# Spacing the steps of a side stream by their bytes, and six groups of an MLP block as seven half products

## The chip, the cores and the metric

The kernel runs on one core of a Trainium2 chip. The metric is the device time of one launch, in microseconds (us). Three runs of the kernel before took 3230.37, 3218.70 and 3221.98 us, a median of 3221.98.

## The reference

One inference step of a one-layer decoder. A prompt of 2048 tokens and 64 sampled tokens (8 sequences of 8) go through one input projection, two kinds of heads (softmax attention with forget gates, "fox", and a matrix memory, "mLSTM"), one output projection, a layer norm, an MLP and a second layer norm. The sampled tokens attend to 8192 cached positions per sequence, which lie in pages that a page table picks. All data are float32.

```python
z = x @ w_in                                     # 1024 -> 3600 columns: q, k, v, gates
fox = softmax(q k^T / 8 + forget sums) v         # prompt: causal; sampled: cache pages + new tokens
mix = concat(fox, mlstm) @ w_o
x1  = layer_norm(2**0.25 * x + mix)
hid = square(relu(x1 @ w1))                      # 1024 -> 4096
y   = layer_norm(2**0.25 * x1 + hid @ w2)        # 4096 -> 1024
```

## The kernel before

**Products.** A float32 product is made of three passes: both operands are split into a high part (ScalarE copy, line 149) and the rest (a subtraction, line 152, on VectorE unless another engine is named), and `mm3` (lines 157 to 159) issues high x high, low x high and high x low as three matmuls into the same sum. `mm2` (163, 164) is the form for the 64 sampled tokens, whose high and low parts lie side by side.

**Phases in order.** A: input projection in four blocks of 512 tokens, with the mLSTM beside it. B: prompt attention. O: output projection and first norm. C: the MLP.

**Phase C** goes through tokens in four blocks of 512 (`CB`); the last also has the 64 sampled tokens. A block goes through the 4096 hidden columns in 16 groups of 256. `hidden(fc)` computes one group's activations for the block (2 x 8 x 3 matmuls of 128x512, banks named `ph`), `output(fc)` multiplies the group before with its 256 rows of w2 (4 token tiles x 2 column halves x 2 x 3 matmuls of 128x512, banks named `py`) and VectorE adds every 128x512 result onto the running rows `y` (line 1638). Groups 14 and 15 are output together. Each group needs four 512 KB pieces of weights (`wr`, four buffers): two of w1, two of w2. The fourth block is done by `last_block` with `seven` (groups 0 to 13): the 512 x 256 activations and the 256 x 1024 weights are cut into halves each way, and the 2x2 product of halves is made from seven products instead of eight. One product is 2 token tiles x 3 matmuls of 128x512. `sums` builds sums and differences on GpSimd (lines 1714 to 1723), `build` splits them, and `output` adds each result to the quarters of `y` that it belongs to, on VectorE (1771 for the part that is shared and kept in `ac`, 1778 for the rest); `join` adds `ac` once at the end.

**The stream.** Attention of the sampled tokens to the cache (`sample_attention`) is a generator of 295 steps that runs beside phases A, O and C. Every matmul of the main work adds its nominal time to a counter by `tick`; when the counter passes a pace, one step is issued (`attend`). The pace is 5.6 in phase A (`PACE_A`), infinite in B (six gathers are issued there by hand), 5 in O and C (`PACE_C`). A step may hold: `k_gather` (512 KB of keys through an indirect DMA issued by GpSimd, line 2027), `k_turn` (two VectorE transposes, 2033), `qk_step` for every fourth step (32 small matmuls, `sQ`, 2056), a pair of `v_gather`s (2 x 512 KB of values, 2145) and `pv_step` (16 small matmuls, `sO`, 2169). Keys come in steps up to 255; from 35 on values come too, one pair per two steps; from 256 on, values alone. Steps up to NA+2 belong to phase A, with NA = 4 x GA and GA = 19, and use a ring of four key pieces; later ones use a ring of six. At most two pairs of values are held, one of them in the landing buffers `xr` of the MLP.

In the third block, after group 13's hidden part and group 12's output, whatever is left of the stream is issued at once, and `sampled()` follows: the output projection and first norm of the 64 sampled tokens, which needs the stream's result (`mhs` is its split input; products by `mm2`).

**Order.** The program order above is not the final one: a scheduler with its own timing model orders the instructions of each engine at build time. `tc.issue_after(x)` keeps what is issued under it behind x in that order.

## Time and profile before

| what | us |
|---|---|
| median of three runs | 3221.98 |
| the profiled execution | 3218.31 |
| its span, first to last instruction | 3216.6 |
| TensorE busy in it | 3159.1 |
| VectorE, ScalarE, GpSimd busy | 2202.3, 1381.0, 1013.6 |

The profile is of one execution. PE is TensorE's matmul side, PEld its weight loads, DVE is VectorE, ACT ScalarE, POOL GpSimd, SP the queue that issues most transfers. "L1638" is a line of the kernel. Matmuls overlap, so the shown duration of one (0.39 us for 128x512) is longer than its distance to the next; the distance is what it costs. In the span phase A lasts to about 890 us, B to about 1290, O to about 1530, the first three blocks of C to about 2810, the last to the end.

### The profile page before, as it was taken

The page shows a single profiled execution, that of the slowest core. Times are in us where ns is not written, and L with a number is a line of the kernel's source. Part 1 is how long each engine was busy: PE and PEld are TensorE (multiplying, and loading weights), DVE is VectorE, ACT ScalarE, POOL GpSimd, SP SyncE. Part 2 cuts the span into 40 slices and gives each one's busy share as a digit, 9 for nine tenths or more (in the row PEclk, how much of TensorE's full clock was granted, in tenths as well). Part 3 has the DMA queues.
Part 4 walks back from the last instruction along what each step waited for, and adds up shares of the span by engine and source line. Part 5 has one row for each costly group of instructions (what it writes and reads, how often), then busy time and mean ns, then how long its engine had stood idle before and what let it go on. Part 6 is the DMA issues. An engine that isn't in the chain of part 4 may idle for free.

```text
span 3216.6 us, 54583 instructions
## 1 busy us (share of the span) xinstructions
PE 3159.1 (98%) x20140; PEld 2546.2 (79%) x20140; DVE 2202.3 (68%) x5111; ACT 1381.0 (43%) x2675; POOL 1013.6 (32%) x1157
## 2 busy tenths in 40 slices
PE   9999999999999999999999999999999999999998
PEld 8988787787777777777777777777777777799997
DVE  6857667567577777776566667666676544787777
ACT  4444245345377777412333333233423333444443
POOL 0011122323244444354333223333233110164441
PEclk9999999999999999999999999999999999999999
DMA  6565775977642324688877768677678655432221
GB/s 192 163 193 174 226 225 172 311 253 236 213 133 86 80 85 118 235 308 281 293 254 251 252 243 309 249 247 253 238 263 295 206 175 168 149 132 83 89 92 56
DMA packets 413731, 641.86 MB, mean 200 GB/s; under 512 B 82908, under 2 KB 295200, under 8 KB 412568
## 3 DMA queue, kind: packets, MB, share of 16 engines
q1 hardware_dynamic: 337208, 360.99, 36.6%
q0 software_dynamic: 74304, 270.57, 22.7%
q10 hardware_dynamic: 1952, 6.82, 0.6%
q8 instruction: 159, 2.61, 0.3%
q14 instruction: 108, 0.88, 0.1%
HBM read 585.43 MB, written 52.83 MB: 198 GB/s over the span
## 4 chain that ended last, share of the span: by engine, by line
PE 37%; issue 7%; DMA 3%; POOL 2%; DVE 2%; ACT 0%; DVEq 0%; POOLq 0%; ACTq 0%
PE ph L159 6%; PE ph L157 6%; PE ph L158 6%; PE py L157 5%; PE py L159 5%; PE py L158 5%; DMA kT<-cache_k,idxK 3%; PE sO L2169 2%; PE sQ L2056 1%; POOL kT L2027 1%; DMA vt<-cache_v,idxV 1%; PE py L163 0%; PE py L164 0%; POOL vt L2145 0%; PE sT L2128 0%
## 5 line engine op out<-in xcount | busy, mean ns | idle before, releaser
L149 ACT ACTIVATE wh<-wr 128x1024 fp32r<-128x1024 f32 x268 | 277.8, 1056 | 537.9 <-PE py L159 254.4
L2027 POOL DMA_INDIRECT kT<-cache_k,idxK x256 | 265.6, 1037 | 733.0 <-PE sQ L2056 609.6
L2033 DVE STREAM_TRANSPOSE kT<-kT 128x512 f32<-128x512 f32 x512 | 329.4, 685 | 194.6 <-DMA kT<-cache_k,idxK 194.4
L157 PE MATMUL ph<-x1h,wh 128*128 128x512 f32 (+2 forms) x1280 | 453.1, 354 | 3.3 <-ACT x1h L149 1.9
L158 PE MATMUL ph<-x1l,wh 128*128 128x512 f32 (+2 forms) x1280 | 452.3, 354 | 1.0 <-DVE x1l L152 1.0
L159 PE MATMUL ph<-x1h,wl 128*128 128x512 f32 (+2 forms) x1280 | 450.6, 354 | 2.0 <-DVE wl L152 1.9
L152 DVE TENSOR_TENSOR wl<-wr,wh 128x1024 fp32r<-128x1024 f32 x252 | 308.5, 1233 | 81.9 <-PE ph L159 45.7
L157 PE MATMUL py<-wh,h 128*128 128x512 f32 (+1 forms) x888 | 348.2, 397 | 3.6 <-DVE y L1638 3.3
L158 PE MATMUL py<-wl,h 128*128 128x512 f32 (+1 forms) x888 | 347.6, 392 | 0.0
L159 PE MATMUL py<-wh,h 128*128 128x512 f32 (+1 forms) x888 | 346.4, 391 | 0.1
L1638 DVE TENSOR_TENSOR y<-y,py 128x512 f32<-128x512 f32 x336 | 223.0, 677 | 178.8 <-PE py L159 177.7
L157 PEld LDWEIGHTS ph<-x1h,wh 128*128 128x128 f32 x1280 | 241.5, 189 | 37.4 <-ACT x1h L149 2.1
L159 PEld LDWEIGHTS ph<-x1h,wl 128*128 128x128 f32 x1280 | 241.3, 189 | 36.6 <-DVE wl L152 3.2
L158 PEld LDWEIGHTS ph<-x1l,wh 128*128 128x128 f32 x1280 | 241.4, 189 | 36.4 <-issue 2.5
L2145 POOL DMA_INDIRECT vt<-cache_v,idxV x160 | 161.4, 1009 | 306.9 <-PE sO L2169 257.4
L157 PE MATMUL pm<-whi,xhT 128*128 128x512 f32 (+2 forms) x648 | 235.2, 365 | 2.5 <-DVE xlT L152 1.0
L158 PE MATMUL pm<-wlo,xhT 128*128 128x512 f32 (+2 forms) x648 | 229.6, 354 | 0.0
L159 PE MATMUL pm<-whi,xlT 128*128 128x512 f32 (+2 forms) x648 | 229.2, 354 | 0.0
L157 PEld LDWEIGHTS py<-wh,h 128*128 128x128 f32 x888 | 166.6, 188 | 50.3 <-issue 9.9
L159 PEld LDWEIGHTS py<-wh,h 128*128 128x128 f32 x888 | 166.7, 188 | 36.8 <-issue 2.1
L158 PEld LDWEIGHTS py<-wl,h 128*128 128x128 f32 x888 | 167.0, 188 | 32.3 <-issue 2.1
L149 ACT ACTIVATE whi<-wra 128x1024 fp32r<-128x1024 f32 (+1 forms) x112 | 119.0, 1062 | 150.6 <-PE pm L159 100.7
(490 smaller groups left out, 6965.8 us busy)
## 6 DMA issues: line engine op xcount, KB each, us to landing
wr<-w SPq DMA_DIRECT2D x256, 512.0 KB
wra<-w_in SPq DMA_DIRECT2D x112, 512.0 KB
Rb<-dR SPq DMA_DIRECT2D x128, 128.0 KB
wr<-w_o SPq DMA_DIRECT2D x16, 512.0 KB
xr<-dmix SPq DMA_DIRECT2D x16, 512.0 KB
y<-x_prompt SPq DMA_DIRECT2D x16, 512.0 KB
dx<-y SPq DMA_DIRECT2D x16, 512.0 KB
qn<-dq SPq DMA_DIRECT2D x120, 64.0 KB
```

Source lines behind the costliest of these rows:

```text
L149: last["ACT"] = A.activation(dst, src, AF.Copy, scale=scale)
L152: r = (eng or V).tensor_tensor(dst, src, hi.bitcast(F32), op=OP.subtract)
L157: T.matmul(ps, wh, xh, start=first, stop=False, skip_group_check=free)
L158: T.matmul(ps, wh, xl, start=False, stop=False, skip_group_check=free)
L159: last["PE"] = T.matmul(ps, wl, xh, start=False, stop=stop, skip_group_check=free)
L1638: V.tensor_tensor(y, y, ps, op=OP.add)
L2027: G.indirect_dma_start(out=piece(n), out_offset=None, in_=ck, in_offset=IO(ap=idxK[:, b, j // 2, j % 2:j % 2 + 1], axis=0))
L2033: V.transpose(x, x)
L2056: r = T.matmul(pq[h4 * 32:h4 * 32 + 32, hg].rearrange("p (k f c) -> p k f c", k=2, f=4), z["qb"][:, hd], kv, start=(db == 0), stop=(db == ...
L2145: vx["last"] = G.indirect_dma_start(out=vt.rearrange("p f c -> p (f c)"), out_offset=None, in_=cv, in_offset=IO(ap=idxV[:, b, (kt % 4) * 4 ...
L2169: after_ = T.matmul(po[r:r + 32], z["PT"][:, hg, 2 * f + g, pg].rearrange("p h q -> p (h q)"), vts[f][:, g, hg * 256:(hg + 1) * 256], star ...
```

## The change

Five things are changed.

1. *Spacing.* In phase A the pace is 3.6 while the step number is below 34 (`PACE_K`, keys alone) and 6.0 afterwards. GA is 21, so eight more steps (79 to 86) belong to phase A. From step 262 (`TAIL`) the pace is 2.3 (`PACE_T`), up to four pairs of values are held (the key ring's three places are used for them too), and a step gathers at most one pair more than is held.
2. *Where the stream must end.* The left-over steps are issued after group 6's hidden part and group 5's output in the third block instead of seven groups later; `sampled()` follows one group later.
3. *Seven products.* Groups 8 to 13 of the third block go through `seven`. Group 8's hidden part has both subtractions of w1 on VectorE (`eng` None); in groups 9 to 13 the second is on GpSimd.
4. *Banks.* From group 8 on, the third block's sums are in the six banks that before were opened by `last_block` (three pairs, `ppl`), its hidden part and the transposes at the seam to the last block are in the two banks `sX` and `sO` that the stream used.
5. *Small.* The first operations of phase B (`b_first`, on GpSimd) are placed behind the matmul issued last; the last addition of the sampled tokens' first norm is on VectorE, not GpSimd; an unused argument goes.

```diff
-PACE_A = 5.6
+PACE_A = 6.0
+PACE_K = 3.6
 PACE_C = 5
+SEVEN = 8
+PACE_T = 2.3
...
-        while acc[1] is not None and acc[0] > acc[2]:
-            acc[0] -= acc[2]
+        while acc[1] is not None and acc[0] > (pace := PACE_T if kx["tail"] else PACE_K if kx["keys"] else acc[2]):
+            acc[0] -= pace
             attend()
...
-                    b_first()
+                    with tc.issue_after(last["PE"].ins):
+                        b_first()
...
             for fc in range(16):
+                if ci == 2 and fc == SEVEN:
+                    break
...
-                if fc == 13 and ci == 2:
+                if ci == 2 and fc == SEVEN - 2:
                     while acc[1] is not None:
                         tick(100.0)
-                    sampled()
+            if ci < 2:
+                continue
+            run = seven(ph, blk, ys, C["x"], w2, lambda: es_l["ppl"])
+            sampled()
+            run["hidden"](SEVEN, None)
+            run["sums"](SEVEN)
+            output([SEVEN - 1])
+            es.close()
+            es_l["ppl"] = es_q.enter_context(tc.tile_pool(name="ppl", bufs=1, space=PSUM, reuse_waits="tile"))
+            for n in range(SEVEN + 1, 16):
+                if n < 15:
+                    h = run["build"](n - 1)
+                if n < 14:
+                    run["hidden"](n)
+                    run["sums"](n)
+                else:
+                    hidden(n, lambda f: pps.tile([128, 512], F32, name="ph", tag="sO" if f else "sX", bufs=1))
+                if n < 15:
+                    run["output"](n - 1, *h)
+                if n == 14:
+                    run["join"]()
...
+            load(3, px_of)
+            output([14, 15], True)
...
-    GA = 19
+    GA = 21
...
+    def v_place():
+        free = [0] + ([1] if vx["more"] else []) + ([2, 3, 4] if kx["tail"] else [])
+        return next((p for p in free if p not in vx["live"]), None)
...
-        if n > NA + 2:
+        if kx["tail"]:
+            pairs = min(len(vx["live"]) + 1, 4)
+        elif n > NA + 2:
             pairs = (2, 0, 1, 0)[n % 4]
...
+    TAIL = 262
...
+        kx["tail"], kx["keys"] = n >= TAIL, n < 34
         step(n)
```

More of the change, by code (lines that the diff above doesn't have):

```diff
@@ L105, in body @@
     vx = dict(more=None, live=[], next=0, of={})
-    kx = dict(ring=None, new=False, free=False)
+    kx = dict(ring=None, new=False, free=False, tail=False, keys=False)
     def take_back():
@@ L1623, in output @@
                     pss = []
+                    pair = es_l["ppl"].tile([128, 2, 512], F32, name="py", bufs=3) if wide else None
                     for hf, cs in enumerate(halves):
@@ L1626, in output @@
                             todo = halves if both else [cs]
-                            new = [ppc.tile([128, 512], F32, name="py", bufs=3) for _ in todo]
+                            new = [ppc.tile([128, 512], F32, name="py", bufs=3) for _ in todo] if pair is None else [pair[:, i] for i in range(2)][hf:hf + len(todo)]
                             pss += new
@@ L1663, in phase_c, with px_of @@
                         SY.dma_start(v, dap(I[f"ln2_{x}"], 0, [[0, 128], [1, D]]))
+            es_px.close()
+            C["px"] = es_px.enter_context(tc.tile_pool(name="px", bufs=1, reuse_waits="tile"))
+            C["w"] = 576
+            turn = [0]
+            def px_of():
+                turn[0] += 1
+                return pps.tile([128, 4, 128], F32, name="px2", tag="sO" if turn[0] % 2 else "sX", bufs=1)
+            load(3, px_of)
+            output([14, 15], True)
         es_h.close()
-        es.close()
-        last_block(w2, gb2)
+        last_block(w2, gb2, es_l["ppl"])
+        es_q.close()
         es_px.close()
@@ L2139, in v_gather @@
         vx["next"] += 1
-        place = 0 if 0 not in vx["live"] else 1
+        place = v_place()
         vx["live"].append(place)
```

42 lines of the change are left out of this document (20 added, 22 removed).

## The prediction

> **What bounds the kernel.** First I read the busy shares, then who TensorE waited for, then single stretches.
>
> ```profile
> span 3216.6 us, 54583 instructions
> PE 3159.1 (98%) x20140; PEld 2546.2 (79%) x20140; DVE 2202.3 (68%) x5111; ACT 1381.0 (43%) x2675; POOL 1013.6 (32%) x1157
> ```
>
> ```profile
> PE sO L2169 <- DMA vt<-cache_v,idxV: 4.6, 4, 2.4
> PE py L163 <- DVE mhs L152: 1.8, 1, 1.8
> PE ph L157 <- ACT wh L149: 1.4, 1, 1.4
> ```
>
> TensorE is without work for 3216.6 - 3159.1 = 57.5 us in all. The second view (who waits for whom: total, times, longest) shows that this is many small pieces; the whole stream costs it 4.6 us of waiting for values. So time comes from removed matmuls, almost one for one, and little else can come back. The stretches in which the third block and the end of the stream lie say the same (TensorE busy, then the other engines, clock, share of the DMA engines, GB/s):
>
> ```profile
> 2400.00:2480.00 80.00, 80.00 (x512) 61.81 (x511) 57.18 (x107) 28.77 (x40) 32.29 (x30) 1.00 0.93 339
> 2640.00:2720.00 80.00, 80.00 (x425) 62.87 (x424) 36.75 (x46) 24.32 (x33) 8.82 (x9) 1.00 0.53 176
> ```
>
> What one matmul costs is read from the timeline, from the first to the last of 18 in a row:
>
> ```profile
> 2448.09 0.39 PE L157 MATMUL py<-wh,h 128*128 128x512 f32 x1
> ...
> 2451.94 0.39 PE L159 MATMUL py<-wh,h 128*128 128x512 f32 x1
> ```
>
> 3.85 us over 17 distances is 0.2265 us each.
>
> **1. Seven products.** A plain group's output is 4 tiles x 2 halves x 2 x 3 = 48 such matmuls; by seven products it is 7 x 2 x 3 = 42. Six groups lose 36 matmuls: 36 x 0.2265 = **-8.2 us**. A group shrinks from 96 to 90 matmuls, 21.7 to 20.4 us. The sums, splits and additions that come in lie on the other engines, and they cost nothing as long as these keep up with 20.4 us. Their prices, from the last block, which works this way already, over four of its groups, and from the third block as it is:
>
> ```profile
> 2910.39 3.37 SPq L1706 DMA_DIRECT2D wr<-w  x2
> ...
> 2983.22 3.36 SPq L1706 DMA_DIRECT2D wr<-w  x2
> ```
> ```profile
> L1778 DVE TENSOR_TENSOR y<-y,py 128x512 f32<-128x512 f32 (+1 forms) x53 | 36.9, 733 | 5.6 <-PE py L159 5.6
> L152 DVE TENSOR_TENSOR wl<-wr,wh 128x1024 fp32r<-128x1024 f32 x12 | 14.8, 1234 | 10.8 <-PE ph L159 9.9 <-PE py L164 0.9
> L152 DVE TENSOR_TENSOR tl<-kT,th 128x1024 fp32r<-128x1024 f32 x8 | 10.9, 1360 | 0.0
> L1771 DVE TENSOR_TENSOR kT<-kT,py 128x1024 f32<-128x1024 f32 x4 | 4.9, 1222 | 3.6 <-PE py L159 3.6
> L152 DVE TENSOR_TENSOR h<-sr,h 128x1024 fp32r<-128x1024 f32 x4 | 4.9, 1216 | 0.0
> L152 DVE TENSOR_TENSOR h<-xr,h 128x256 fp32r<-128x256 f32 (+1 forms) x8 | 4.1, 550 | 0.0
> ```
> ```profile
> L1638 DVE TENSOR_TENSOR y<-y,py 128x512 f32<-128x512 f32 x39 | 26.8, 686 | 41.5 <-PE py L159 41.1
> ...
> L152 DVE TENSOR_TENSOR h<-hq,h 128x512 fp32r<-128x512 f32 x10 | 6.9, 693 | 10.6 <-ACT h L149 10.6
> ```
>
> VectorE per new group: 12 additions x 0.686 = 8.2; the shared part 1.2; weight rests 2 x 1.23 and one of half width 0.6; `tl` 2 x 1.36 = 2.7; activations 1.22 + 2 x 0.55 = 2.3. Together 17.5 of 20.4 us, 86% (a plain group by the same rows: 8 x 0.686 + 4 x 1.23 + 2 x 0.69 = 11.8). The last block's group takes (2983.22 - 2910.39)/3 = 24.3 us and shows no idle TensorE. So there is room, but 2.9 us of it. Collisions can eat that:
>
> ```profile
> 2807.28 3.22 DVE L152 TENSOR_TENSOR wl<-wr,wh 128x1024 fp32r<-128x1024 f32 x1
> ```
> ```profile
> 2807.05 2.38 POOL L152 TENSOR_TENSOR wl<-wr,wh 128x1024 fp32r<-128x1024 f32 x1 [0.80 <-ACT wh L149]
> ```
> ```profile
> 2810.56 0.39 PE L159 MATMUL ph<-x1h,wl 128*128 128x256 f32 x1 [1.90 <-DVE wl L152]
> ```
>
> At the last block's beginning a subtraction of VectorE that takes 1.23 us elsewhere took 3.22 beside one of GpSimd, 2.0 more, and TensorE stood 1.9 us. In the new groups GpSimd works in the third block too. I take +1 for all six groups and the pipeline's filling at group 8, with bounds 0 (the last block's steady part) and +7 (two collisions a group: 17.5 + 4.0 = 21.5, 1.1 us over, six times).
>
> The Trainium skill, GPSIMD Engine Reference, section 1 (Specifications), says the two engines share their path to SBUF and contend when VectorE has two SBUF inputs. The two rows agree. By that rule alone every subtraction of such a group could be stretched; by the ratio of the rows 1360 and 1216 ns that makes 1 us a group, and the sum stays.
>
> **2. The end of the stream.** TensorE's share of the stream is the same, only earlier. It must fit: before, steps 79 to 294 at pace 5 take 1080 nominal us, and phase O plus C up to group 12's output offers 32 x 5.1 + 2 x 327.7 + 276.5 = 1095. Afterwards steps 87 to 261 at 5 and 33 at 2.3 take 951, and up to group 5's output there are 163.2 + 655.4 + 133.1 = 952. So one or two steps are left for the forced issue, and they hold no matmul of weight. The bytes: 1 MB a step and two step times before, 0.5 MB per tail step. A tail step lasts 2.3 x 0.2265/0.2133 (the tick's own value) = 2.4 us and half a `pv_step`,
>
> ```profile
> 2603.82 1.05 PE L2169 MATMUL sO<-xr,PTs 128*32 128x256 f32 x16
> ```
> ```profile
> DMA to landing us min/median/max: 4.5/8.1/9.3
> ```
>
> so 2.9 us: 172 GB/s for the gathers, where a step before brings 1 MB in 5 x 1.06 + 0.9 (a quarter of `sQ` and two `pv_step`s) = 6.2 us, 160. No new load, except at its beginning: steps 262 to 265 each gather a pair, and the second of them (step 263) is used in step 266, 3 x 2.9 = 8.7 us later. Values land 8.1 us after issue in this part (second line: minimum, median, maximum of the value gathers of 2400 to 2560), at most 9.3, and the queue of gathers ahead adds to it. I take **+1**, bounds 0 and +6 (a stall of 2.4 us and what follows it, below).
>
> **3. `sampled()`.** It stood behind the stream's last result:
>
> ```profile
> 2703.58 0.62 PE L2175 MATMUL sO<-vns,PTn 8*32 8x256 f32 x4
> ```
> ```profile
> 2739.09 0.39 PE L163 MATMUL py<-wh,mhs 128*128 128x256 f32 x1 [1.76 <-DVE mhs L152]
> 2747.64 0.50 PE L157 MATMUL ph<-x1h,wh 128*128 128x512 f32 x1 [1.45 <-ACT wh L149]
> ```
>
> Now a whole group (hidden 7, output 6) lies between, so the wait of 1.76 us goes: **-1.8**. The 1.45 us are the four weight buffers that `sampled` had filled with w_o; that stays, and with group 8 holding two of the four for its w2 it may double: bounds -3.2 and +3. The new banks and the seam to the last block: same work, two banks for the transposes in place of three; 0, bounds -2 (the 1.9 us above) and +3. The removed and moved norm operations and `b_first` were not waited for by TensorE: 0.
>
> **4. Phase A.** Four key steps in the first part took, by GpSimd's gathers,
>
> ```profile
> 351.43 0.99 POOL L2027 DMA_INDIRECT kT<-cache_k,idxK  x1 [27.36 <-DVE st L711]
> 355.21 0.94 POOL L2027 DMA_INDIRECT kT<-cache_k,idxK  x1 [0.30 <-issue]
> 388.21 1.25 POOL L2027 DMA_INDIRECT kT<-cache_k,idxK  x1 [0.15 <-issue]
> ```
> ```profile
> 396.70 1.31 DVE L2033 STREAM_TRANSPOSE kT<-kT 128x512 f32<-128x512 f32 x2 [7.25 <-DMA kT<-cache_k,idxK]
> ```
> ```profile
> 348.47 0.64 PE L2056 MATMUL sQ<-kT,qb 128*32 128x256 f32 x8
> 349.63 1.50 PE L2056 MATMUL sQ<-kT,qb 128*32 128x256 f32 x24
> ```
> ```profile
> DMA to landing us min/median/max: 4.3/8.4/10.5
> ```
>
> 36.8 us from one four to the next, at 4 x 5.6 nominal, so 1.64 real per nominal; at 3.6 it is 23.7. A ring of four needs in turn: four gathers issued (355.21 + 0.94 - 351.43 = 4.7), the last one's landing (8.4, at most 10.5 here), its transposes (1.3) and `sQ` (349.63 + 1.50 - 348.47 = 2.7): 17.1 to 19.2. It fits, and 32 matmuls of `sQ` cost what they did. The eight steps that come into A leave C: 0. One stall may go or come, with its consequence:
>
> ```profile
> 784.71 1.12 PE L2169 MATMUL sO<-vt,PTs 128*32 128x256 f32 x16 [2.40 <-DMA vt<-cache_v,idxV]
> ```
> ```profile
> 780.00:790.00 10.00, 7.60 (x43) 5.06 (x42) 4.35 (x9) 7.43 (x22) 5.73 (x10) 0.78 0.62 214
> 790.00:800.00 10.00, 10.00 (x47) 8.23 (x46) 8.48 (x21) 5.33 (x13) 3.43 (x6) 0.88 0.93 287
> ```
>
> Behind 2.4 idle us the granted clock was 0.78 and 0.88, so 2.2 + 1.2 = 3.4 us more were lost: 5.8 for one late pair. This place has the loads for phase B beside it before and after; wider spacing (6.0) helps it, a new alignment may hurt. I take **0**, bounds -5.8 and +5.8.
>
> The Trainium skill, TensorE: Matmul & The Clock Gate, Part 1, has the clock fall after an idle window of about 3.4 us. The trace differs: 2.4 us were enough here. By the rule a stall shorter than that costs itself alone: the bound would be 2.4 in place of 5.8, and the slow rival below would end at 3228.
>
> **Sum** against the profiled execution, 3218.3: -8.2 + 1 + 1 - 1.8 + 0 = -8.0, 3210.3. The median of the runs shown is 3.7 us higher, 3222.0, which gives 3214. I predict **3212**, 0.3% under that median. About 0.5%, 16 us, is what a measurement of this kernel can tell from no change.
>
> **Rivals.** *Eaten by VectorE.* For it: 86% and the collision; against it: no idle TensorE in the last block at (36.9 + 14.8 + 10.9 + 4.9 + 4.9 + 4.1)/98 us = 78%. It gives +7 instead of +1 in part 1: 3216 to 3220. *Stalls go as well.* The 784 stall, both waits around `sampled` and the one at 2810 go: -5.8 - 1.4 - 1.9 and the two +1 not needed, about 11 more: 3201 to 3205. For it: all are single events that hang on alignment; against it: their causes (loads of phase B, four weight buffers) remain. *Slower: the key steps of phase A.* If landing under the denser gathers exceeds 23.7 - 8.7 = 15.0 us, each four waits, VectorE's queue stands behind the transposes and TensorE with it; from a landing of 17 us on it is 2.0 a four, 16 us for eight fours, and with the slow clock behind each (3.4) 43: 3228 to 3255. Against it: 10.5 is the longest landing there, and the DMA engines are far from full. *Late values in the tail,* at every second step rather than once: 8 x 2 us, 3226; against it: from step 270 on pairs are gathered seven or eight steps ahead.
>
> **Chances.** Forecast 0.50 (3206 to 3217); eaten 0.18; late values 0.06: all within 0.5%, together 0.74. Stalls go as well 0.18, faster by over 0.5%. Slow phase A, or a cause of its kind that I do not see, 0.08, slower. The range for 8 in 10 goes from 3202, inside the stalls' case, to 3226, the end of the late values.
>
> **What would show it.** Matmuls named `py` of 128x512 in the third block fewer by 36, groups 9 to 13 spaced 20.4 us; no `mhs` wait; idle TensorE of about 55 us in all; key fours in A1 some 24 us apart with TensorE busy; at step 266 at most one wait for `vt`. The forecast is wrong if groups 9 to 13 take 21.5 us or more, if the clock falls at new places, or if the sum of TensorE's waits moves by more than 10 us.

## The result, and the profile after

The changed kernel took 3253.88 us (median of 6 runs, 3250.19 to 3258.2), the kernel before beside it 3229.05 (6 runs, the three shown above among them, 3218.7 to 3232.33): a ratio of 1.0078, 95% interval 1.0067 to 1.0088. It is 0.8% slower, where 3212 us, a ratio of 0.997 to the median of then, was forecast. The profiled execution took 3253.62 us.

The first view is the head of the page, as shown of before:

```profile
span 3251.9 us, 54593 instructions
PE 3168.4 (97%) x20104; PEld 2547.2 (78%) x20104; DVE 2246.7 (69%) x5160; ACT 1394.5 (43%) x2694; POOL 1089.2 (33%) x1209
```

TensorE is without work for 83.5 us instead of 57.5. It is also 9.3 us longer at work with 36 fewer matmuls, 8.2 us' worth. A lower granted clock accounts for up to 12.3 us of these 17.5 (see the clock below); the other 5 are open. The second view gives stretches by phase: length, busy time of TensorE, its weight loads, VectorE, ScalarE and GpSimd, then the clock, the DMA engines' share and GB/s. Before:

```profile
0.00:891.80 891.80, 867.91 (x5559) 714.64 (x5559) 588.88 (x1609) 381.43 (x883) 197.42 (x240) 0.99 0.70 214
1310.80:1511.20 200.40, 198.24 (x1269) 152.46 (x1269) 139.89 (x275) 48.63 (x65) 104.03 (x94) 1.00 0.86 302
1511.20:2360.50 849.30, 842.08 (x5377) 649.72 (x5376) 559.86 (x1061) 292.79 (x453) 265.06 (x277) 1.00 0.73 258
2360.50:2808.20 447.70, 444.06 (x2581) 348.62 (x2580) 273.57 (x438) 160.62 (x231) 99.80 (x93) 1.00 0.61 209
```

These are phase A (to the first `pS` product of B), phase O (from the first `pw` product), the first two blocks of C (a block begins with the transposes `px` of its input), and the third block with the seam to the last one. The seam is the stretch from the first transposes for the last block to that block's first product. The same after, and behind them the seam alone and a stretch of the seven products:

```profile
0.00:918.30 918.30, 884.98 (x5694) 721.64 (x5694) 604.40 (x1641) 381.87 (x885) 222.92 (x256) 0.99 0.70 218
1338.60:1543.20 204.60, 200.34 (x1270) 153.56 (x1270) 139.57 (x275) 48.77 (x65) 104.86 (x94) 0.99 0.85 297
1543.20:2395.90 852.70, 844.79 (x5430) 651.59 (x5429) 564.46 (x1073) 291.98 (x452) 269.19 (x281) 1.00 0.73 259
2395.90:2844.90 449.00, 430.76 (x2356) 337.95 (x2354) 310.31 (x452) 177.07 (x251) 156.13 (x128) 0.98 0.55 187
2811.20:2844.90 33.70, 23.40 (x119) 18.69 (x118) 30.16 (x42) 12.33 (x19) 16.00 (x10) 0.89 0.35 118
...
2680.00:2782.00 102.00, 102.00 (x448) 83.75 (x447) 82.76 (x98) 48.72 (x65) 50.84 (x40) 1.00 0.37 114
```

The seam before, for comparison, had no idle time and the full clock:

```profile
2781.30:2808.20 26.90, 26.90 (x139) 22.00 (x138) 22.82 (x34) 10.88 (x17) 10.22 (x7) 1.00 0.29 106
```

Stream work moved between the phases, and has to be taken out first. Its price, from the groups of instructions in phase A after (busy time, mean ns of one, idle time before them):

```profile
L2088 PE MATMUL sQ<-kT,qb 128*32 128x256 f32 x672 | 47.2, 390 | 0.7 <-ACT PTs L2161 0.7
L2209 PE MATMUL sO<-vt,PTs 128*32 128x256 f32 x384 | 31.3, 385 | 2.4 <-DMA vt<-cache_v,idxV 2.4
```

That is 0.070 us for an `sQ` and 0.082 for an `sO`. Phase A has 64 more of each after the change (+9.7 us), the first two blocks 32 and 16 more (+3.6), the third block 96 and 80 fewer (-13.3). What is left:

| stretch | longer by | moved work | matmuls saved | lost |
|---|---|---|---|---|
| A | 26.5 | +9.7 | | 16.8 |
| B | 1.3 | | | 1.3 |
| O | 4.1 | | | 4.1 |
| C, blocks 1 and 2 | 3.4 | +3.6 | | -0.2 |
| C, block 3 and seam | 1.3 | -13.3 | -8.2 | 22.8 |
| C, block 4 | -1.4 | | | -1.4 |

The sum, 35.3 us, is the difference of the two spans. It is more than the 24.8 us between the medians, because the profiled execution of before (3218.3) lies at the lower end of its runs. So two places carry the loss: phase A, and the third block with its seam. Of the 16.8 us in A, 9.4 are idle time (33.3 against 23.9) and 3.4 a lower clock. Of the 22.8 in the third block, 14.0 stand in the seam (10.3 idle, 3.7 by the clock), 6.4 at the stream's end and 1.7 in the clock behind the wait at `mhs`; the last two are read below.

Who TensorE waited for (total, times, longest):

```profile
PE sO L2209 <- DMA vt<-cache_v,idxV: 9.9, 6, 3.3
...
PE ph L160 <- DVE x1l L155: 4.7, 1, 4.7
PE px L1435 <- issue: 4.0, 1, 4.0
PE mm L1032 <- DVE nq L1025: 3.9, 2, 2.2
PE mr L451 <- DVE gnat L438: 3.3, 1, 3.3
...
PE px L385 <- ACT st L605: 2.9, 1, 2.9
PE mn L912 <- DVE kw L905: 2.3, 1, 2.3
...
PE py L166 <- DVE mhs L155: 1.8, 1, 1.8
```

Three kinds are new. In phase A the small products of the mLSTM (`mm`, `mr`, `mn`) wait for VectorE. The stream waits 9.9 us for values instead of 4.6. At the seam two waits of 4.0 and 4.7 us stand within 7 us, in TensorE's timeline (start, duration, what, in brackets the idle time before it):

```profile
2833.68 0.60 PE L1435 MATMUL px<-ident,y 128*128 128x128 f32 x4
2838.26 0.66 PE L1435 MATMUL px<-ident,xr 64*128 64x64 f32 x4 [3.98 <-issue]
2839.48 0.69 PE L1435 MATMUL px<-ident,xr 64*128 64x64 f32 x4 [0.56 <-DVE x1l L155]
2844.91 0.82 PE L160 MATMUL ph<-x1h,wh 128*128 128x320 f32 x2 [4.74 <-DVE x1l L155]
```

After 2833.7 only the transposes of the sampled tokens are left, and the last block's first product needs them split by VectorE. For the wait of 3.98 us the profile names no releaser; it ends 0.1 us after the subtraction at 2837.48, which empties a bank of the transposes. VectorE is busy for 30.16 of the seam's 33.70 us. Two of its instructions, at 2831.25 and 2841.73, are stretched beside GpSimd's subtractions, which began before them; the subtraction at 2839.95, which began 0.19 us ahead of GpSimd's, is not:

```profile
2831.25 3.33 DVE L155 TENSOR_TENSOR wl<-wr,wh 128x1024 fp32r<-128x1024 f32 x1
...
2837.48 0.68 DVE L155 TENSOR_TENSOR x1l<-px,x1h 128x512 fp32r<-128x512 f32 x1
...
2839.95 1.20 DVE L155 TENSOR_TENSOR wl<-wr,wh 128x1024 fp32r<-128x1024 f32 x1
...
2841.73 2.70 DVE L211 SCALAR_TENSOR_TENSOR y<-y,ln,g 128x1024 f32<-128x1024 f32 x1
```
```profile
2831.11 2.39 POOL L155 TENSOR_TENSOR wl<-wr,wh 128x1024 fp32r<-128x1024 f32 x1
2840.14 3.22 POOL L155 TENSOR_TENSOR wl<-wr,wh 128x1024 fp32r<-128x1024 f32 x1 [6.64 <-ACT wh L152]
```

### The profile page after: what moved, and what is told of

Read it like the earlier page. It is cut to its first block, busy times and chain, and to the rows that moved or that the text cites. A ratio compares the mean times of both kernels' runs of the same rounds, so it can differ in the third digit from the quotient of the medians.

```text
span 3251.9 us, 54593 instructions
## 1 busy us (share of the span) xinstructions
PE 3168.4 (97%) x20104; PEld 2547.2 (78%) x20104; DVE 2246.7 (69%) x5160; ACT 1394.5 (43%) x2694; POOL 1089.2 (33%) x1209
## 4 chain that ended last, share of the span: by engine, by line
PE 43%; DMA 3%; DVE 2%; issue 2%; POOL 1%; ACT 0%; DVEq 0%; POOLq 0%; ACTq 0%
PE ph L160 7%; PE ph L162 7%; PE ph L161 7%; PE py L160 6%; PE py L162 6%; PE py L161 6%; PE sO L2209 2%; DMA vt<-cache_v,idxV 2%; PE sQ L2088 2%; DMA kT<-cache_k,idxK 1%; PE py L166 1%; PE py L167 1%; PE sT L2160 0%; POOL kT L2059 0%; DVE wl L155 0%
## 5 line engine op out<-in xcount | busy, mean ns | idle before, releaser
L2059 POOL DMA_INDIRECT kT<-cache_k,idxK x256 | 277.1, 1082 | 746.0 <-PE sQ L2088 603.9
L152 ACT ACTIVATE wh<-wr 128x1024 fp32r<-128x1024 f32 (+1 forms) x268 | 276.2, 1047 | 482.2 <-PE py L162 209.8
L155 DVE TENSOR_TENSOR wl<-wr,wh 128x1024 fp32r<-128x1024 f32 (+1 forms) x247 | 305.3, 1242 | 89.3 <-PE ph L162 57.3
L160 PE MATMUL py<-wh,h 128*128 128x512 f32 x828 | 327.0, 397 | 3.3 <-DVE y L1643 2.0
L161 PE MATMUL py<-wl,h 128*128 128x512 f32 x828 | 324.0, 392 | 0.0
L162 PE MATMUL py<-wh,h 128*128 128x512 f32 x828 | 323.1, 392 | 0.5 <-DVE h L155 0.5
L1643 DVE TENSOR_TENSOR y<-y,py 128x512 f32<-128x512 f32 x288 | 191.3, 677 | 143.3 <-PE py L162 142.1
L160 PEld LDWEIGHTS py<-wh,h 128*128 128x128 f32 x828 | 155.6, 188 | 45.5 <-issue 9.1
L1811 DVE TENSOR_TENSOR y<-y,py 128x512 f32<-128x512 f32 (+1 forms) x245 | 163.7, 710 | 36.3 <-PE py L162 36.1
L162 PEld LDWEIGHTS py<-wh,h 128*128 128x128 f32 x828 | 155.3, 188 | 36.1 <-issue 3.7
L155 DVE TENSOR_TENSOR wlo<-wra,whi 128x1024 fp32r<-128x1024 f32 (+1 forms) x112 | 138.9, 1241 | 64.6 <-ACT whi L152 62.2
```

The source lines that it names most:

```text
L152: last["ACT"] = A.activation(dst, src, AF.Copy, scale=scale)
L155: r = (eng or V).tensor_tensor(dst, src, hi.bitcast(F32), op=OP.subtract)
L160: T.matmul(ps, wh, xh, start=first, stop=False, skip_group_check=free)
L161: T.matmul(ps, wh, xl, start=False, stop=False, skip_group_check=free)
L162: last["PE"] = T.matmul(ps, wl, xh, start=False, stop=stop, skip_group_check=free)
L1643: V.tensor_tensor(y, y, ps, op=OP.add)
```

## The experiments

Each ratio is to the kernel before, run on the same chip in the same set. The runs came in five sets: the 1st to 4th experiment, 5th to 8th, 9th to 12th, 13th to 16th, and the last two, on which before took 3229.14, 3284.69, 3230.56, 3281.44 and 3300.88 us. In the edits, "..." stands for lines that are not shown. In the second, fourth and fifth set the first two blocks of C took 20 to 46 us more each than in the other sets, whatever the edit, so there a kernel's ratio and its other stretches are read, not its time.

**First set: the parts, one at a time.**

1. Phase A as before; the same stream end, so the rest of it closer.

```diff
-PACE_A = 6.0
+PACE_A = 5.6
...
-PACE_C = 5
+PACE_C = 4.77
...
-    GA = 21
+    GA = 19
...
-        kx["tail"], kx["keys"] = n >= TAIL, n < 34
+        kx["tail"], kx["keys"] = n >= TAIL, False
```

> The changed kernel with phase A's stream as before (pace 5.6 throughout, GA 19, so 79 steps in phase A); phases O and C at pace 4.77 so that the stream still ends at group 6 of the third block. Theory A (phase A's denser and more numerous steps make VectorE stand behind late key gathers and TensorE behind VectorE, some 19 us): phase A ends near 892 us as before (918 in the changed kernel, of which 8 us are moved work), the time falls by 15 to 20 us to 3234 to 3240. Rival (the loss in phase A is from b_first's new place or from chance alignment, not from spacing and number): phase A keeps 10 us or more of the loss, the time stays above 3244. The denser pace in phases O and C may cost up to 4 us.

Measured: 3248.61 us, ratio 1.0060 (1.0045 to 1.0076). Phase A ends at 893.6, where it was:

```profile
0.00:893.60 893.60, 867.14 (x5558) 714.41 (x5558) 588.91 (x1609) 380.84 (x883) 201.38 (x240) 0.99 0.69 214
```

But O and the first two blocks of C take 208.2, 432.2 and 437.9 us, against 200.5, 420.4 and 428.9 before: 28.5 more, of which 96 `sQ` and 80 `sO` moved there make 13.3. So 15.2 us are lost there, 11.3 more than in the changed kernel (4.1 - 0.2), in place of the 16.8 in A. Phase A's loss is that of the stream there, and not of the place of `b_first`, which stayed; and a stream put closer costs in C too. The whole time did not fall to the 3234 to 3240 us that the theory expected.

2. Groups 8 to 13 plain, in before's banks, with before's seam (three banks for the transposes, no `join`); the rest as changed. The loop goes through all 16 groups again, and the part for the seven products behind it goes out.

```diff
-                if ci == 2 and fc == SEVEN:
-                    break
...
-            run = seven(ph, blk, ys, C["x"], w2, lambda: es_l["ppl"])
...
-            load(3, px_of)
-            output([14, 15], True)
...
```

> The changed kernel with groups 8 to 13 of the third block in the plain form and the seam to the last block as before (three banks for the transposes, no join); the stream is that of the changed kernel and still ends at group 6. Theory B (the seam costs 14 us because join and two banks put TensorE behind VectorE there): 8.2 us come back as matmuls, the seam's 10 idle us and its slow clock go, so the time falls by 4 to 8 us, to 3247 to 3251. Rival (the seam's stall comes from the stream's new end or from the weight buffers): the seam stays slow and the time rises by 8 us to 3261.

Measured: 3247.68 us, ratio 1.0062 (1.0047 to 1.0078). The third block with its seam takes 440.4 us instead of 449.0, though it has 36 matmuls (8.2 us) more, and the seam has no idle time; the last block takes 3.0 us more. So the form of the seven products and their seam cost 8.6 + 8.2 - 3.0 = 13.8 us there, for the 8.2 that they save.

3. `join` on GpSimd.

```diff
-                    V.tensor_tensor(ys[t][:, d], ys[t][:, d], a, op=OP.add)
+                    (V if more else G).tensor_tensor(ys[t][:, d], ys[t][:, d], a, op=OP.add)
```

> The changed kernel with the third block's six join additions on GpSimd in place of VectorE. If VectorE's backlog of 4 us from join is what delays the last transposes' evictions at the seam, the seam shrinks by 4 to 10 us and the time falls as much, to 3244 to 3250. If the two banks or the late landing buffers alone set it: no change (3252 to 3255).

Measured: 3257.84 us, ratio 1.0092 (1.0076 to 1.0107); the seam's idle time is 11.0 us. The join is not what delays it.

4. `mhs` in buffers of its own.

```diff
-            mhl = ph.tile([128, 8, 128], F32R, name="mhs", tag="h", bufs=4)
+            mhl = ps_.tile([128, 8, 128], F32R, name="mhs", tag="S", bufs=4)
```

> The changed kernel with the split input of the sampled tokens' projection (mhs) in a buffer of its own instead of one of the four h buffers. If the 1.76 us wait is for an h buffer that group 6's output holds: the wait goes, 1.8 us and the slow clock behind it (1.7) with it, the time falls by 2 to 4 us. If it is for the stream's result, as the prediction had it: the wait stays, no change.

Measured: 3256.52 us, ratio 1.0084 (1.0070 to 1.0097). The 1.76 us wait is gone, so the cause was right: `mhs` took its turn in the four buffers of `h`. But other waits of TensorE came in its place, 0.69 us at 2645.3 and 1.34 at 2648.1, and 1.7 us were lost to the clock behind the second. So of the 1.76 + 1.7 us there nothing is left to see in the whole time.

**Second set: causes inside phase A and the seam.**

5. Three banks for the seam's transposes (the third from a pair of the last block's).

```diff
+                if turn[0] % 3 == 0:
+                    return es_l["ppl"].tile([128, 2, 512], F32, name="py", bufs=3)[:, 0].rearrange("p (k c) -> p k c", k=4)
-                return pps.tile([128, 4, 128], F32, name="px2", tag="sO" if turn[0] % 2 else "sX", bufs=1)
+                return pps.tile([128, 4, 128], F32, name="px2", tag="sO" if turn[0] % 3 == 1 else "sX", bufs=1)
```

> The changed kernel with one edit: the transposes of x1's sums at the seam rotate over three banks (the two that the change gives them, and half of a pair of the last block's banks) instead of two. Theory A (the seam's 10 us of idle time and 3.7 us of clock come from the two banks: TensorE's next transpose waits until VectorE has emptied a bank, and VectorE is late): the stretch from the third turn of the loop to the last block's first hidden product loses 4 to 10 us of idle time, and the time falls from 3253.9 to about 3245 to 3250. Rival B (VectorE's own backlog sets it: some 20 us of work between 2815 and 2850 us, whatever the banks): the stretch stays within 2 us and the time with it. The edit also moves instructions of TensorE there, so a change of under 3 us in the whole decides nothing; the idle time of the stretch does.

Measured: ratio 1.0088 (1.0067 to 1.0108). The seam's idle time is 7.5 us instead of 10.3, a new wait of 2.94 us of group 15's hidden part for a bank among it. The third block with its seam takes 447.6 us, where the next two kernels of this set take 458.3 and 458.2, but the last block takes 416.4 against their 408.6 and 408.4: 34 matmuls of the third block (7.7 us) went behind its beginning. In the whole time nothing is won.

6. No GpSimd in the last block's first group.

```diff
-            w1p = w1_pieces(n, eng)
+            w1p = w1_pieces(n, None if more and n == 0 else eng)
```

> The changed kernel with one edit: the weight subtractions of the last block's first group run on VectorE instead of GpSimd, on which two of VectorE's instructions at the seam lay beside GpSimd's (3.33 us where such a one takes 1.22, 2.70 where it takes 1.27). Theory A (that overlap delays VectorE at the seam by 3 to 4 us): the two instructions fall to about 1.3 us, VectorE takes on some 1.2 us each for those it takes over, and the first hidden product of the last block comes 1 to 3 us earlier than 2844.9 us. Rival B (the overlap is not on the path): the first hidden product stays within 1 us, or comes later by the 2 to 3 us of added work on VectorE. In the whole time either is at the limit of what 5 rounds tell: 3250 to 3256.

Measured: ratio 1.0095 (1.0075 to 1.0115). The seam is 32.8 us with 9.6 idle (33.7 and 10.3 in the changed kernel). VectorE's subtraction of 3.33 us is gone and a norm operation of 2.76 us stays; the waits stay too. The overlap is about a microsecond of the seam.

7. The turning of gathered keys in phase A one step later.

```diff
-        g, r = divmod(n - 2, 4)
+        g, r = divmod(n - 3, 4)
         if 0 <= g < GA and r >= 2:
             k_turn(4 * g + 2 * r - 4)
```

> The changed kernel with one edit: in the first part of the stream (phase A) the four transposes of a group of gathered keys stand one step later behind their gathers. Theory A (VectorE works in order and stands at the eviction of a key pair that has not landed, 116 us of such waits in the second to fourth block of phase A after the change against 81.5 before, and TensorE's chain of small products behind it): the waits on landing fall to under 60 us, phase A ends 8 to 18 us earlier than 918.3 us, and the time falls to 3236 to 3246. Rival B (the loss of 18.6 us in phase A is that of 26 more steps' work on VectorE and TensorE between the chain's products, and not of landing): the waits fall as well, but phase A ends within 4 us of 918.3 and the time stays at 3250 to 3257.

Measured: ratio 1.0092 (1.0073 to 1.0112). VectorE's waits for keys in A's second to fourth block fall from 116 us in the changed kernel to 85, not to under 60 as expected, but about to what they were before it (81.5). Phase A ends at 920.8, where the two kernels above, in the same set, end it at 923.9 and 922.0. So a quarter less of these waits gave 1 to 3 us: late keys are not the main cost.

8. Phase A's steps 5.05 apart throughout.

```diff
-PACE_A = 6.0
+PACE_A = 5.05
...
-        kx["tail"], kx["keys"] = n >= TAIL, n < 34
+        kx["tail"], kx["keys"] = n >= TAIL, False
```

> The changed kernel with one edit: the steps of phase A are all 5.05 us apart instead of 3.6 for the first 34 and 6.0 for the rest; their number stays. Theory A (the number of steps, eight more groups' worth of work on the engines, costs the 18.6 us): phase A ends within 4 us of 918.3 us and the time stays within 4 us of 3253.9. Rival B (the uneven spacing costs it: the first 34 steps come faster than their gathers land): phase A ends 8 to 15 us earlier and the time falls to 3239 to 3247.

Measured: ratio 1.0054 (1.0034 to 1.0075), the best of the set. Phase A ends at 914.0 with the same number of steps in it, 9.0 us ahead of the mean of the 5th and 6th.

**Third set.**

9. Before's number of steps in A, spaced unevenly.

```diff
-PACE_A = 6.0
+PACE_A = 6.7
...
-PACE_C = 5
+PACE_C = 4.77
...
-    GA = 21
+    GA = 19
```

> The kernel of the first experiment (phase A with before's 26 fewer steps, the rest of the stream at 4.77 us) with one difference: phase A's steps are uneven as in the changed kernel, 3.6 us for the first 34 and 6.7 us after, where that one had 5.6 us throughout; the number of steps in phase A is the same within one. Theory (uneven spacing alone costs about half of the loss in phase A): phase A ends 7 to 12 us later than the 893.6 us of the first experiment. Rival (the loss is the number of steps, and uneven spacing is worse only on top of the denser stream): it ends within 4 us of 893.6. The whole time by the theory: a ratio to before of 1.008 to 1.010, by the rival 1.005 to 1.007.

Measured: ratio 1.0095 (1.0077 to 1.0113). Phase A ends at 907.9, with the matmuls of the first experiment (x5559 and x5558) and 14.3 us longer (its row, to be read beside that experiment's):

```profile
0.00:907.90 907.90, 870.20 (x5559) 715.53 (x5559) 591.10 (x1609) 381.17 (x883) 206.87 (x240) 0.99 0.67 210
```

So the uneven spacing costs by itself, without one step more. TensorE is busy 3.1 us longer, and idle 37.7 us (907.90 - 870.20) instead of 26.5.

10. All repairs: even steps in A, `mhs`, more banks (next one), and the 2.3 us spacing only from the seventh of the stream's last steps on, paid for by 4.9 in place of 5 ahead of it.

```diff
-PACE_A = 6.0
+PACE_A = 5.05
...
-PACE_C = 5
+PACE_C = 4.9
...
-        while acc[1] is not None and acc[0] > (pace := PACE_T if kx["tail"] else PACE_K if kx["keys"] else acc[2]):
+        while acc[1] is not None and acc[0] > (pace := PACE_T if kx["fast"] else PACE_K if kx["keys"] else acc[2]):
...
-        kx["tail"], kx["keys"] = n >= TAIL, n < 34
+        kx["tail"], kx["keys"], kx["fast"] = n >= TAIL, False, n >= TAIL + 6
```

> All repairs together: phase A's steps 5.05 us apart throughout, the third block's end with more banks (the next experiment's edit), a buffer of its own for mhs, and the 2.3 us spacing of the stream's end only from its seventh such step on, with 4.9 us ahead of it. If the parts found so far add up (phase A -9, seam -5 to -10, mhs -3.5, the late values at the stream's end -4), the time is 18 to 25 us under the changed kernel's on the same chip: a ratio to before of 0.999 to 1.003. If they don't add up (each stall filled lets the next one show), it stays above 1.004.

Measured: ratio 1.0078 (1.0058 to 1.0098), no better than unrepaired. Phase A ends at 906.0, 17.1 us earlier than in the unedited kernel of this set; but O and the first two blocks of C take 1066.7 instead of 1055.2 us, where 32 `sQ` and 32 `sO` more account for 4.9. So 6.6 us more are lost there, where the pace of 4.9 is what differs, and one pair of values is late all the same (2.65 us). The third block with its seam is 13.1 us shorter, though 18.5 us of work moved out of it (60 matmuls, 13.6 us, went behind the last block's beginning, and the stream's 4.9 ahead); the last block is 15.4 longer. So most of what phase A gave is lost again behind it.

11. More banks at the seam alone.

```diff
-                    hidden(n, lambda f: pps.tile([128, 512], F32, name="ph", tag="sO" if f else "sX", bufs=1))
+                    hidden(n, lambda f, b=[]: (b if f else (b.append(es_l["ppl"].tile([128, 2, 512], F32, name="py", bufs=3)), b)[1])[-1][:, f] if n == 14 else pps.tile([128, 512], F32, name="ph", tag="sO" if f else "sX", bufs=1))
...
+            pair_of = lambda p: (pair.clear(), pair.append(p.tile([128, 2, 512], F32, name="py", bufs=3)), pair[0])[2]
...
-                return pps.tile([128, 4, 128], F32, name="px2", tag="sO" if turn[0] % 2 else "sX", bufs=1)
+                return pps.tile([128, 4, 128], F32, name="px2", tag="sO" if turn[0] % 4 == 1 else "sX", bufs=1) if turn[0] % 2 else (pair_of(es_l["ppl"]) if turn[0] % 4 == 2 else pair[0])[:, turn[0] // 2 % 2].rearrange("p (k c) -> p k c", k=4)
```

> The changed kernel with more banks at the end of the third block: group 14's hidden products go to a pair of the last block's banks, and the transposes of x1's sums rotate over four banks (sO, sX and the halves of such a pair) instead of two. The edit with three banks for the transposes alone moved part of the waiting to group 15's hidden products, which waited 2.94 us for a bank. Theory A (single banks in sO and sX make TensorE wait on VectorE and ScalarE there): the stretch from the third turn to the last block's first hidden product, and the group ahead of it, lose 6 to 10 us of idle time and the clock's loss of 3.7 us; the time falls 6 to 12 us under the changed kernel's on the same chip. Rival B (VectorE's backlog of the join, the norms and the splits is the bound, whatever the banks): idle time moves but the end of the kernel stays within 3 us.

Measured: ratio 1.0117 (1.0099 to 1.0136), the slowest. Idle time moved to other transposes, up to 6.5 us at one of them, and 60 matmuls (13.6 us) of the third block went behind the last block's beginning, which is 15 us longer.

12. The changed kernel again.

> The changed kernel itself once more, unedited, as the base of this set on the same chip. Both theories expect a ratio to before of 1.0067 to 1.0088 as measured, phase A ending within 6 us of 918.3 us, and the seam with 10 us of idle time.

Measured: 3254.3 us, ratio 1.0078 (1.0062 to 1.0095); phase A ends at 923.1, the seam has 10.4 us idle.

**Fourth and fifth set: the seam of the kernel before.**

13. The repairs of the 10th without the banks.

```diff
-PACE_A = 6.0
+PACE_A = 5.05
...
-PACE_C = 5
+PACE_C = 4.9
...
-            mhl = ph.tile([128, 8, 128], F32R, name="mhs", tag="h", bufs=4)
+            mhl = ps_.tile([128, 8, 128], F32R, name="mhs", tag="S", bufs=4)
...
-        kx["tail"], kx["keys"] = n >= TAIL, n < 34
+        kx["tail"], kx["keys"], kx["fast"] = n >= TAIL, False, n >= TAIL + 6
```

> The kernel with all repairs, without that of the seam's banks (which cost 12 us by itself): phase A's steps 5.05 us apart throughout, a buffer of its own for mhs, and 2.3 us spacing only from the seventh step of the stream's end on, with 4.9 us ahead of it. If the 10.8 us that the seam's banks cost in the second place are the only thing that kept the repairs from adding up: a ratio to before of 1.003 to 1.005, against the changed kernel's 1.0078, with phase A ending near 906 us. If the repairs don't add up otherwise: 1.006 or more.

Measured: ratio 1.0095 (1.0068 to 1.0122); phase A ends at 907.9; in the whole time of this set nothing of the repairs is seen. The repairs don't add up, and the banks of the seam were not all that kept them from it.

14. The same with before's seam: after group 13 the pairs are given back, and group 15's hidden part and the transposes go through three banks of a pool with three single banks for the outputs.

```diff
...
-                    run["join"]()
+                    run["join"](), es_q.close(); ppc = es_q.enter_context(tc.tile_pool(name="ppd", bufs=1, space=PSUM, reuse_waits="tile"))
...
-            load(3, px_of)
-            output([14, 15], True)
+            load(3, lambda: ppc.tile([128, 4, 128], F32, name="px2", tag="ph", bufs=3))
+            output([14, 15])
...
```

> The three repairs, and the end of the third block in the form of the kernel before: once group 13's products are out, the last block's pairs of banks are given back, and group 15's hidden products and the transposes of x1's sums rotate over three single banks of a pool of their own, as they did before. Theory (the seam's loss of 14 us is that of the order and the banks, not of VectorE's added work): the idle time between 2,600 us and the last block's first hidden product falls by 8 us or more against the same kernel without this edit, and the ratio to before is 0.999 to 1.002. Rival (VectorE's backlog from the seven products and the join bounds it): the ratio stays within 0.001 of the kernel with three repairs.

Measured: ratio 1.0073 (1.0051 to 1.0095), between what theory and rival expected, and the interval overlaps the 13th's. The third block with its seam, and the last block, in the 13th and then the 14th experiment:

```profile
2449.70:2899.00 449.30, 428.12 (x2287) 335.68 (x2286) 305.77 (x440) 175.98 (x249) 146.48 (x120) 0.99 0.54 180
2899.00:3306.80 407.80, 394.62 (x2360) 359.66 (x2360) 305.44 (x410) 182.83 (x337) 154.27 (x129) 0.98 0.27 87
```
```profile
2448.80:2889.00 440.20, 427.98 (x2289) 336.01 (x2288) 296.57 (x430) 173.00 (x246) 140.53 (x117) 0.99 0.54 179
2889.00:3299.90 410.90, 394.53 (x2359) 358.68 (x2357) 318.03 (x419) 185.25 (x340) 165.83 (x132) 0.99 0.28 92
```

9.1 us less for the same matmuls, 3.1 more in the last block: 6.0 won in these two profiles.

15. That seam in the changed kernel, and nothing else.

> The changed kernel with the seam of the kernel before (the edit of the last one) and nothing else. Theory (order and banks): 3240 to 3247 us where the changed kernel has 3254, a ratio to before of 1.003 to 1.006, and the seam's 10 us of idle time under 4. Rival (VectorE's backlog): 1.007 to 1.009.

Measured: ratio 1.0093 (1.0064 to 1.0122). The seam, by its window and by TensorE's timeline up to the last block's first product:

```profile
2860.80:2888.30 27.50, 27.25 (x140) 22.20 (x139) 22.49 (x34) 10.88 (x17) 10.32 (x7) 1.00 0.26 87
```
```profile
2882.97 0.46 PE L1435 MATMUL px<-ident,xr 64*128 64x64 f32 x4
...
2888.03 0.39 PE L162 MATMUL py<-wh,h 128*128 128x512 f32 x1
2888.25 0.30 PE L160 MATMUL ph<-x1h,wh 128*128 128x320 f32 x1
```

In the changed kernel the seam is 33.7 us with 23.40 busy. Here the last transposes stand 5 us ahead of the first product with output products between them, and VectorE splits their result behind that cover. VectorE's work did not become less: by the lines of the 13th and 14th it is busy for 611.2 and 614.6 us in the two stretches together. So the seam's waits are those of the order that its banks allow, and not of the added work by itself. The whole time does not show it: the ratio is no lower than the rival expected (1.007 to 1.009).

16. Seven products in groups 11 to 13 alone: before's 19 groups of keys and 5.6 us in A, 5 in C, before's seam, `mhs` and the stream's end as in the 14th.

```diff
-PACE_A = 6.0
+PACE_A = 5.6
...
-SEVEN = 8
+SEVEN = 11
...
-    GA = 21
+    GA = 19
...
```

> Seven products in groups 11 to 13 alone (4.1 us less on TensorE, half of the 8.2), so that the stream may end three groups later and needs no closer steps: before's 19 groups of keys and 5.6 us in phase A, 5.0 us after it, the repairs of the stream's end and of mhs, and the seam of the kernel before. Theory (closer steps cost, wherever they stand, and the seam's banks cost): phase A ends within 4 us of before's 891.8 us and the time is 0 to 8 us under before's, a ratio of 0.9975 to 1.000. Rival (the seam keeps its cost with the seven products): 1.002 to 1.004.

Measured: ratio 1.0014 (0.9997 to 1.0032); phase A ends at 891.9, the seam has no idle time. That lies between theory and rival.

17. The 15th again.

> The changed kernel with the seam of the kernel before and nothing else, once more: in the first run the seam's idle time was 0.3 us instead of 10, but the ratio's interval, 1.0064 to 1.0122, was too wide to show it in the whole time. Theory (the seam's form costs some 9 to 14 us): a ratio to before of 1.003 to 1.006. Rival (what the seam gives back is lost again in the last block, whose time was 1 us and whose idle time 3 us longer in that run): 1.007 to 1.009.

Measured: ratio 1.0087 (1.0063 to 1.0111); the seam 27.7 us, 0.5 idle. The whole time does not show the 6 us, in either run; it agrees with the rival, by which the last block loses what the seam gives back (410.7 us against 407.0 in the changed kernel).

18. The 16th again.

> Seven products in groups 11 to 13 alone, with no closer steps in phases A and C, before's seam, and the repairs of mhs and of the stream's end, once more, since the first run's interval, 0.9997 to 1.0032, leaves its sign open. Theory (4.1 us less on TensorE and the stall at mhs gone, with no loss beside them): a ratio to before of 0.997 to 0.999. Rival (the steps of the stream's end, at 2.3 us, cost what the three groups give): 1.000 to 1.003.

Measured: ratio 1.0032 (1.0016 to 1.0047). Not faster than before, in either run; this one is slower, by a little more than the rival expected (1.000 to 1.003). What takes the 4.1 us that TensorE saves there is open: in this set the first two blocks of C, which this edit leaves as they were before, took 80 us more (929.3 against 849.3) than in the profile of before, and no trace of before from these chips is there to compare.

No version was faster than the kernel before.

## Why the prediction was wrong

**Phase A, the term of 0 with bounds of 5.8, was the step that failed**; it measured 16.8. The working asked whether the ring of four keys keeps its turn (17.1 to 19.2 of 23.7 us) and took phase A for unharmed if it does. It does keep it: seven fours in a row begin 22 us apart on average (242.2 to 375.1 us; 17.1 to 28.7 from one to the next), and keys land after 9.4 us, at most 12.2. What waits is another chain. Four levels of where phase A ends tell it apart:

| phase A | ends at, us |
|---|---|
| before's spacing, 4 kernels (before, 1st, 16th, 18th) | 891.8 to 893.6, mean 892.4 |
| before's number of steps, uneven (9th) | 907.9 |
| eight more steps, even (8th, 10th, 13th, 14th) | 904.6 to 914.0, mean 908.1 |
| eight more steps, uneven (ten profiles with A as in the changed kernel) | 916.5 to 923.9, mean 920.6 |

From the first row to the last, 28.2 us, 9.7 are work moved there. The uneven spacing costs 12.5 (last row less third) or 15.5 (second less first); the rest, 6.0, is what the steps cost when they stand closer at all. Profiles of the same phase A scatter by 7 to 9 us, so these sizes are rough; the ranges of the rows do not overlap, except those of the 9th and of the even steps, which differ in their number.

The loss stands in one stretch. Here are the same 540 matmuls of the projection (`pm`, from the 1441st on), before and after:

```profile
291.30:458.10 166.80, 163.93 (x899) 126.07 (x898) 112.30 (x302) 60.01 (x141) 31.37 (x35) 0.99 0.76 228
```
```profile
288.30:482.40 194.10, 182.79 (x1056) 136.68 (x1056) 129.83 (x349) 71.35 (x175) 48.78 (x51) 0.96 0.72 226
```

That is 27.3 us longer, of which 96 `sQ` and 32 `sO` more make 9.3: 18.0 us are lost here, all that phase A loses. TensorE is idle for 11.3 us instead of 2.9, and the clock is lower. Between the 9th and the 1st experiment the same matmuls take 184.9 and 163.9 us, 13.0 more beyond the moved work, of the 14.3 in all; with even steps (8th) they take 170.7. The second half of the 34 dense steps is gathered in this stretch. The first half, from 242 us on, cost nothing, so density alone is not the whole condition.

The slow rival named phase A and the right sign, but its mechanism, keys that land too late, is not the one: it asked for a landing of more than 15.0 us, and the 7th experiment took most of the added waits for keys away. That 3253.88 us lies within its 3228 to 3255 is luck, since phase A gives 16.8 us of it and the third block the rest. Four of the five waits of TensorE over 1.5 us in this stretch stand at the mLSTM's dependent products (`mm`, `mn`, mostly behind VectorE), between which VectorE turns the stream's keys; that this is the whole chain of the cause is read from the waits and was not tried by itself.

**"The new banks and the seam to the last block", a 0 with bounds -2 and +3, was the other.** The seam measured 10.3 us idle and 3.7 us of clock in the changed kernel, none of either before. The prediction counted banks (two in place of three) and not what the order loses with them: which work is left to stand behind the last transposes. The 2nd, 14th and 15th experiments show that place; the 3rd and 6th that neither VectorE's join nor the overlap with GpSimd explains it, the 5th and 11th that more banks in another order do not give the time back. What it costs in the whole time stays open: 6.0 us by the profiles of the 13th and 14th, whose ratios overlap, and nothing that the ratios of the 15th and 17th show.

**Seven products: -8.2 was right,** and the +1 was not needed. In the stretch of 102 us TensorE was busy for 102.00, VectorE for 82.76 (81%, 86% forecast). It holds 448 matmuls, so 90 of them, a group, take 20.5 us (20.4 forecast); w2's issues, two a group, stand 21.6 and 19.6 us apart:

```profile
2699.24 6.72 SPq L1739 DMA_DIRECT2D wr<-w  x2
...
2720.81 4.69 SPq L1739 DMA_DIRECT2D wr<-w  x2
...
2740.42 5.43 SPq L1739 DMA_DIRECT2D wr<-w  x2
```

The rival that VectorE eats it did not come.

**The end of the stream: +1 was short.** Two late pairs came, 1.47 us at 2428.7 and 3.26 at 2443.7, at the beginning of the stream's end as the prediction had it, and a stretch at a low clock behind the second:

```profile
2443.74 1.07 PE L2209 MATMUL sO<-vt,PTs 128*32 128x256 f32 x16 [3.26 <-DMA vt<-cache_v,idxV]
```
```profile
2440.00:2450.00 10.00, 6.74 (x56) 4.18 (x46) 3.87 (x12) 1.06 (x2) 8.00 (x8) 0.83 1.03 398
2450.00:2460.00 10.00, 10.00 (x45) 8.22 (x45) 5.98 (x8) 5.31 (x8) 1.69 (x2) 1.00 1.02 413
```

1.47 + 3.26 + 0.17 x 10 = 6.4 us, a little over its upper bound of 6. After that none is late, so the rival of late values at every second step did not come (its 3226 adds 16 us to 3210, and not to the 3212 of the forecast). The first pair landed 10.3 us after its last gather began, 1.0 over the longest that the prediction had read. The second landed after 8.9, as read, but was issued late: the gather ahead took GpSimd 4.86 us, where most take 0.94, beside instructions of VectorE without a break, three subtractions among them:

```profile
2429.63 4.86 POOL L2180 DMA_INDIRECT vt<-cache_v,idxV  x1 [3.26 <-PE sO L2209]
```
```profile
2430.12 3.49 DVE L155 TENSOR_TENSOR wl<-wr,wh 128x1024 fp32r<-128x1024 f32 x3
```

The prediction had no term for how long a gather takes to issue. That VectorE's instructions stretched it is read from these rows and was not tried.

**The `mhs` wait: -1.8 did not come.** The prediction took it for a wait for the stream's result; it is one for a buffer of `h`, and with that buffer apart it went (4th). The 1.45 us behind it, which "stays", is not in this profile.

**The clock** fell at new places, and behind shorter waits than the 2.4 us that the prediction read. The wait at `mhs`, and the two stretches of 10 us around it:

```profile
2638.65 0.39 PE L166 MATMUL py<-wh,mhs 128*128 128x256 f32 x1 [1.76 <-DVE mhs L155]
```
```profile
2630.00:2640.00 10.00, 8.24 (x41) 6.73 (x39) 6.97 (x10) 2.71 (x4) 0.00 (x0) 0.98 0.28 76
2640.00:2650.00 10.00, 10.00 (x66) 9.61 (x66) 9.40 (x13) 5.11 (x5) 0.00 (x0) 0.85 0.84 262
```

1.76 us of idle time were followed by 0.2 + 1.5 us lost to the clock. The Trainium skill, TensorE: Matmul & The Clock Gate, Part 1, puts the fall at an idle window of about 3.4 us; the trace differs here too. But not every such wait is followed by a fall. The same 1.76 us at `mhs` stand in 14 of the profiles; behind five of them the clock fell, behind nine, that of before among them, it did not, and a wait of 2.69 us in before (at 2354.17) had no fall behind it either. Where the clock fell, a second wait of 0.75 to 1.45 us that the other nine have some 8 us later was gone. So the 3.4 us that the prediction adds to a late pair are not sure to come. In all, the clock took 12.3 us more than before: 28.0 us against 15.7, one less the granted clock, summed over the span.

Two of the forecast's own signs named this outcome: "if the clock falls at new places", and "if the sum of TensorE's waits moves by more than 10 us". It moved by 26.0.

## What to carry to other kernels

Work of another chain that is fed in between can cost by how densely and how unevenly it stands, even when its own transfers keep up: look for the dependent chains of small products that share its engines, and space the feed evenly. Before a late stage is given fewer or other banks, list what stands in the order between the last producer's result and its first reader; here that cover hid VectorE's latency, and banks and order changed together. A saving of 8 us that makes a side stream end some 150 us earlier (seven groups of 21.7 us) has to be priced at both ends.

## What the runs showed of the hardware

An idle time of 1.76 us was followed by a fall of the clock in five of 14 profiles. Where a VectorE subtraction of 128x1024 and one of GpSimd overlapped, the one that began later took longer: VectorE's 3.33 us when it began 0.14 us behind (170 others in the same profile, with nothing of GpSimd beside them, took 1.18 to 1.23), GpSimd's 3.22 instead of 2.39 when it began 0.19 us behind, VectorE's then 1.20. Each set ran on a chip of its own, and on three of the five the kernel before itself took 51 to 72 us more than on the other two. In the first two blocks of C TensorE's idle time was 57.3 us in the 17th experiment and 7.9 in the changed kernel, for the same 5430 matmuls:

```profile
1543.80:2474.60 930.80, 873.50 (x5430) 665.70 (x5429) 564.29 (x1074) 292.38 (x452) 265.73 (x281) 0.97 0.68 238
```

TensorE's waits for VectorE's additions into `y` (L1643) are 17.1 us there, against 2.0 in the changed kernel. What differs on those chips stays open.
